# Four short unread products behind each row of 1/rms, the first products by halves of K, and a last scaling that reads its row from the bank

## The chip, the cores and the metric

The kernel runs on one core of one Trainium2 chip. The metric is the device time of one execution in microseconds, from the first to the last instruction with the little that lies around them. Times of single instructions come from one profiled execution, in microseconds from the start of its span.

## The reference, cut to what matters

The input is a sequence of 256 tokens of width 1024. It passes through two layers of a first block and one layer of a second block. Each layer has a mixer between two feed-forward stages or ahead of one. All of them open with the same thing, a root-mean-square norm followed by a matrix product:

```python
def rmsnorm(x, w):
    y = xf * lax.rsqrt(jnp.mean(xf * xf, axis=-1, keepdims=True) + EPS) * w

def swiglu(h, w_gu, w_down):
    gate, up = jnp.split(h @ w_gu, 2, axis=-1)
    return (jax.nn.silu(gate) * up) @ w_down

for layer in range(DEPTH):                      # first block, DEPTH = 2
    x = x + 0.5 * swiglu(rmsnorm(x, ...), ...)
    x = x + mixer(rmsnorm(x, ...))              # gated delta rule, then windowed attention
    x = x + 0.5 * swiglu(rmsnorm(x, ...), ...)
x = rmsnorm(x, final_norm)
# second block: retention and latent attention, merged by two sigmoid gates, then a feed-forward stage
h = h + _mixer(_rmsnorm(h, ...)); h = h + _swiglu(_rmsnorm(h, ...)); return _rmsnorm(h, norm_final_w)
```

There are five feed-forward stages, all with 2,816 inner columns: 22 + 22 blocks of 128 gate and up columns, then 8 blocks of the down matrix over 22 blocks of K (the weight arrays `gu10`, `gu20`, `gu11`, `gu21`, `gu30`).

## The kernel before, in words

The activations lie transposed: 8 tiles `X[0..7]` of 128 features by 256 tokens. Every big product is computed in three parts, for precision: weights and activations are each split into a high part, cast to a narrower format, and a low part, the remainder, and `lin` (lines 373 to 375) issues high by high, low weight by high, high weight by low, for each of the 8 blocks of K. One "column" below is such a set of 24 products (8 x 3), each with 128 x 128 weights loaded and 256 token columns streamed. A feed-forward stage has 44 columns of gate and up and 8 x 66 products of the down matrix, some 1,580 products in all.

A `Stream` brings the weights: `load` starts one transfer of up to 2,048 elements a partition (1 MB, two columns) on SP's queue into one of three buffers, `piece` splits 512 elements of it (half a column) into `whi` on ScalarE (line 355) and `wlo` on VectorE (line 356), with eight buffers of each. `Norm.add` does the same for the activations: `xh` on ScalarE (line 394), `xl` on VectorE (line 395); `accum` squares a tile on ScalarE (403, 406) and adds it up on GpSimd (407).

The norm's factor 1/rms is the same for all features, so it is applied behind the products. `rnorm_nat` sums the squares over the partitions with products that have one column (line 413), VectorE scales them (426), GpSimd takes the power -0.5 (383). `row_bcast` spreads the result over 128 partitions with a product with an identity (435), and VectorE copies it to the tile `r` (437). The next readers are the two multiplications that take a gate and an up column out of their banks (lines 478 and 480).

`opening` orders this for one stage: most of columns a and b, the sums of squares, the rest of a and b, the first block of column c, `row_bcast`, the rest of column c. Seven stages open like this, the first feed-forward stage with other cut points. The banks: pool `ps` has three, pool `pm` five; a feed-forward column takes one of `ps` and gives it back when line 478 or 480 has read it.

The first stage loads the activations in pairs of tiles and its first column in two pieces of half a column. The squares are taken in `squares` after all of the eight `add`. At the end, `row_bcast` gives `r` and three multiplications (line 1534) scale the output tiles, each followed by its transfer.

## Time and profile before

| | |
|---|---|
| median of 3 runs | 1466.39 us (1466.23 to 1467.72) |
| the profiled execution's own time | 1458.11 us |
| its span | 1456.3 us |
| TensorE busy | 1426.7 us, 98% |
| VectorE, ScalarE, GpSimd busy | 1106.2, 858.5, 116.3 us |
| mean granted TensorE clock | 0.995 of full speed |

The busy time counts each product from its start to its modelled end, and products overlap. So the pace of the products is read from the number that start in a stretch, not from the busy share. The profiled execution lies 8.3 us below the median of the runs.

### The profile page before, as it was taken

Reading aid. Unit: us, or ns where it says so; the run is one execution under the profiler, and the core shown is the slowest. Engines: PE = TensorE matmul, PEld = TensorE weight load, DVE = VectorE, ACT = ScalarE, POOL = GpSimd, SP = SyncE. Lnnn points to the kernel's source line nnn. Section 1 sums busy time; section 2 is a strip of 40 time slices with the busy share of each in tenths; the row PEclk is TensorE's granted clock in tenths of the full one; section 3 lists DMA queues with packets and bytes.
Section 4 is the critical chain, followed back from the end, with each engine's and each line's share of the span. In section 5 each row is a group of like instructions: output and inputs, shape, how many; then the busy total and the mean of one; then the engine's idle time right before and its main releaser. Section 6 shows DMA issues by size and latency. Waiting matters only on the chain.

```text
span 1456.3 us, 31032 instructions
## 1 busy us (share of the span) xinstructions
PE 1426.7 (98%) x12318; PEld 1396.2 (96%) x12318; DVE 1106.2 (76%) x2340; ACT 858.5 (59%) x1767; POOL 116.3 (8%) x136
## 2 busy tenths in 40 slices
PE   8999999998999999999999999999999999999997
PEld 8999999998999999999998899999999899999997
DVE  6877667896877766777668877788887868777764
ACT  6555558555655555555556665566545766665552
POOL 2000131011200001000010100013001000100000
PEclk9999999999999999999999999999999999999999
DMA  7655443541456555555552455555333425555551
GB/s 253 227 200 197 159 169 116 169 155 44 156 192 203 186 194 199 184 194 203 188 189 88 145 200 182 198 197 180 123 139 109 145 98 200 197 202 192 189 198 59
DMA packets 46369, 248.35 MB, mean 171 GB/s; under 512 B 11408, under 2 KB 16272, under 8 KB 17168
## 3 DMA queue, kind: packets, MB, share of 16 engines
q1 hardware_dynamic: 45680, 245.87, 49.5%
q8 instruction: 97, 1.59, 0.4%
q10 hardware_dynamic: 544, 0.50, 0.1%
q14 instruction: 48, 0.39, 0.1%
HBM read 243.99 MB, written 2.36 MB: 169 GB/s over the span
## 4 chain that ended last, share of the span: by engine, by line
PE 87%; DVE 7%; ACT 3%; DMA 1%; issue 1%; POOL 1%; SPq 0%; DVEq 0%; POOLq 0%; ACTq 0%
PE bank L373 26%; PE bank L375 26%; PE bank L374 26%; DVE wlo L356 2%; ACT whi L355 1%; DVE cv L652 1%; PE bank L979 1%; PE bank L830 1%; PE bank L1331 1%; PE bank L1136 0%; PE bank L1361 0%; DVE xl L395 0%; PE bank L969 0%; POOL rr L383 0%; DMA xt<-xt 0%
## 5 line engine op out<-in xcount | busy, mean ns | idle before, releaser
L356 DVE TENSOR_TENSOR wlo<-raw,whi 128x512 fp32r<-128x512 f32 x922 | 641.6, 700 | 254.2 <-ACT whi L355 252.7
L355 ACT CAST whi<-raw 128x512 fp32r<-128x512 f32 x922 | 565.5, 619 | 430.4 <-PE bank L375 406.1
L373 PE MATMUL bank<-xh,whi 128*128 128x256 f32 (+1 forms) x2488 | 695.1, 279 | 1.7 <-ACT whi L355 1.0
L374 PE MATMUL bank<-xh,wlo 128*128 128x256 f32 (+1 forms) x2488 | 690.8, 278 | 2.0 <-DVE wlo L356 2.0
L375 PE MATMUL bank<-xl,whi 128*128 128x256 f32 (+1 forms) x2488 | 690.4, 278 | 1.0 <-DVE xl L395 0.9
L373 PEld LDWEIGHTS bank<-xh,whi 128*128 128x128 f32 x2488 | 466.8, 188 | 4.0 <-issue 1.8
L374 PEld LDWEIGHTS bank<-xh,wlo 128*128 128x128 f32 x2488 | 467.0, 188 | 3.2 <-DVE wlo L356 2.8
L375 PEld LDWEIGHTS bank<-xl,whi 128*128 128x128 f32 x2488 | 466.6, 188 | 2.1 <-DVE xl L395 1.6
L375 PE MATMUL bank<-al,whi 128*128 128x256 f32 x880 | 242.9, 276 | 0.0
L373 PE MATMUL bank<-ah,whi 128*128 128x256 f32 x880 | 242.9, 276 | 0.0
L374 PE MATMUL bank<-ah,wlo 128*128 128x256 f32 x880 | 242.9, 276 | 0.0
L373 PEld LDWEIGHTS bank<-ah,whi 128*128 128x128 f32 x880 | 165.2, 188 | 0.0
L374 PEld LDWEIGHTS bank<-ah,wlo 128*128 128x128 f32 x880 | 165.2, 188 | 0.0
L375 PEld LDWEIGHTS bank<-al,whi 128*128 128x128 f32 x880 | 165.2, 188 | 0.0
L407 POOL TENSOR_TENSOR ssq<-sq,ssq 128x256 f32<-128x256 f32 (+1 forms) x72 | 62.9, 874 | 1066.3 <-ACT sq L406 1056.7
L378 ACT CAST ah<-ffu 128x256 fp32r<-128x256 f32 x110 | 44.8, 407 | 26.4 <-DVE ffu L482 26.3
L482 DVE TENSOR_TENSOR ffu<-ffg,ffu 128x256 f32<-128x256 f32 x110 | 46.7, 425 | 4.7 <-ACT ffg L481 1.2
L481 ACT ACTIVATE ffg<-ffg 128x256 f32<-128x256 f32 x110 | 45.4, 414 | 4.0 <-DVE ffg L478 3.7
L478 DVE TENSOR_TENSOR ffg<-bank,r 128x256 f32<-128x256 f32 x110 | 46.6, 424 | 0.9 <-PE bank L375 0.8
L480 DVE TENSOR_TENSOR ffu<-bank,r 128x256 f32<-128x256 f32 x110 | 46.6, 424 | 0.1
L379 DVE TENSOR_TENSOR al<-ffu,ah 128x256 fp32r<-128x256 f32 x110 | 46.0, 418 | 0.6 <-ACT ah L378 0.5
L373 PE MATMUL bank<-dec,whi 128*128 128x256 f32 x128 | 36.8, 287 | 0.0
(368 smaller groups left out, 1429.8 us busy)
## 6 DMA issues: line engine op xcount, KB each, us to landing
raw<-gu SPq DMA_DIRECT2D x109, 1024.0 KB, 4.8
raw<-dn SPq DMA_DIRECT2D x55, 1024.0 KB, 4.8
raw<-wret SPq DMA_DIRECT2D x12, 1024.0 KB, 4.8
raw<-aqk SPq DMA_DIRECT2D x8, 1024.0 KB, 4.7
raw<-wga SPq DMA_DIRECT2D x8, 1024.0 KB, 4.8
raw<-bin SPq DMA_DIRECT2D x6, 1024.0 KB, 4.9
raw<-az SPq DMA_DIRECT2D x4, 1024.0 KB, 4.9
raw<-av SPq DMA_DIRECT2D x4, 1024.0 KB, 5.0
```

Source lines behind the costliest of these rows:

```text
L355: A.copy(hi[:, :n], raw[:, o : o + n])
L356: V.tensor_tensor(lo[:, :n], raw[:, o : o + n], f32(hi[:, :n]), op=ALU.subtract)
L373: mm(o, wh, xh[:, :n], start=k == 0, stop=False)
L374: mm(o, wl, xh[:, :n], start=False, stop=False)
L375: mm(o, wh, xl[:, :n], start=False, stop=k == last)
L378: A.copy(hi, src)
L379: V.tensor_tensor(lo, src, f32(hi), op=ALU.subtract)
L407: G.tensor_tensor(acc[:, :n], q[:, :n], acc[:, :n], op=ALU.add)
L478: V.tensor_tensor(g, pg, r[:, :S], op=ALU.mult)
L480: V.tensor_tensor(u, pu, r[:, :S], op=ALU.mult)
L481: A.activation(g, g, AF.Silu)
L482: V.tensor_tensor(u, g, u, op=ALU.mult)
```

## The change

There are three edits.

First, `settle`: four products with the first 16 of the 128 weight columns of a piece that is split already, and the first activation tile, into a bank that nothing reads. They stand directly behind `row_bcast` in each `opening`, and once more ahead of the gate columns of the second block's mixer, at eight places in all. The first feed-forward stage doesn't use `opening` any more and has none.

Second, the first stage. Its weight chunks are whole (2,048 elements), but the first two are brought in parts, in the order in which they are used. The first three columns are computed by halves of K: the first four blocks of K for the columns 0, 1 and 2, then the last four blocks for each. Then come columns 3, 4 and 5 in banks of `pm`; the squares are spread behind them by one-column copies (`behind`), which only make a square wait for a weight piece. The sums of squares stand in the middle of column 5, and `row_bcast` behind it.

Third, the end. The two halves of the row have a bank each, so that the products of the squares that are there early are all issued ahead of those of the last tile; and the last scaling reads the row from its bank, without the copy to `r`. One small multiplication of constants moves from VectorE to GpSimd.

```diff
+    def settle(st, off, xs):
+        b = bank(pm, [P, 512])
+        wh, _ = st.at(off, P)
+        for i in range(4):
+            mm(b[:16, :S], wh[:, :16], xs[0][0][:, :S], start=True, stop=True)
...
         r = row_bcast(rn, n)
+        settle(*jobs[2][0][1:4])
         c(range(at[1], KD))
...
             if first:
-                first()
-            r = opening(norm, [(pre[i], {}) for i in range(3)], at=(KD - 1, 3) if first else (5, 1))
+                pre = {i: (bank(ps if i < 3 else pm, [P, S]), gu, i * D, norm.xs) for i in range(6)}
+                r = first(lambda i, ks: lin(*pre[i], ks=ks))
...
                 st, stm = Stream("wga"), Stream("wmo")
+                settle(st, 0, xs)
...
+    def first(part):
+        half = range(KD // 2), range(KD // 2, KD)
+        for h in range(2):
+            for i in range(3):
+                for d in half[h]:
+                    if i == 0:
+                        n.add(d, X[d], col("ffn1_norm0", d), square=False)
+                    if d in (0, KD // 2):
+                        gu.piece(2 * i + h)
+        for h in range(2):
+            for i in range(3):
+                part(i, half[h])
+        for h in range(2):
+            part(3 + h, range(KD))
+            for d in half[h]:
+                n.ssq = n.accum(n.ssq, X[d], S, f32(gu.piece((1, 1, 3, 5, 6, 7, 8, 9)[d])[0]))
...
+        part(5, half[0])
+        rn = rnorm_nat(n.ssq, D)
+        part(5, half[1])
+        return row_bcast(rn)
...
-    b = bank(pm, [P, 512])
+    bs = [bank(pm, [P, 512]) for c in range(2)]
+    for i, t in enumerate((fin.ssq, last[0])):
+        for c in range(2):
+            mm(bs[c][:, 0:1], t[:, c * P : c * P + P], ones[:, 0:1], start=i == 0, stop=i == 1)
...
-    r = row_bcast(v)
+    r = bank(pm, [P, 512])
+    for c in range(2):
+        mm(r[:, c * P : c * P + P], v[:, c : c + 1].to_broadcast([P, P]), ident, start=True, stop=True)
```

TensorE at the opening of the second feed-forward stage, before. Names are output<-inputs; `rn` is 1/rms, `bank_5318` the third column:

```order
L375 MATMUL bank_5318<-xl_991_5142,whi_5393 128x256
L435 MATMUL bank_5400<-tabs_81,rn_5376 128x128 x2
L373 MATMUL bank_5318<-xh_993_5148,whi_5393 128x256
L374 MATMUL bank_5318<-xh_993_5148,wlo_5394 128x256
L375 MATMUL bank_5318<-xl_994_5149,whi_5393 128x256
```

The same place in the change, where the third column is `bank_5333`:

```order
L382 MATMUL bank_5333<-xl_990_5157,whi_5408 128x256
L453 MATMUL bank_5415<-tabs_81,rn_5391 128x128 x2
L389 MATMUL bank_5420<-xh_989_5156,whi_5408 16x256 x4
L380 MATMUL bank_5333<-xh_992_5163,whi_5408 128x256
L381 MATMUL bank_5333<-xh_992_5163,wlo_5409 128x256
```

Nothing moved but the four short products, which now stand between the spread of the row and the rest of the column.

VectorE in the first stage around the copy of `r`, before; `bank_162` and `bank_163` are columns 0 and 1:

```order
L426 TENSOR_SCALAR rn_253<-bank_250 128x2
L356 TENSOR_TENSOR wlo_259<-raw_256,whi_258 128x512
L356 TENSOR_TENSOR wlo_280<-raw_256,whi_279 128x512
L437 COPY r_274<-bank_271 128x256
L356 TENSOR_TENSOR wlo_307<-raw_256,whi_306 128x512
L478 TENSOR_TENSOR ffg_295<-bank_162,r_274 128x256
L480 TENSOR_TENSOR ffu_297<-bank_163,r_274 128x256
```

And in the change, where columns 0 and 1 are `bank_126` and `bank_127`:

```order
L444 TENSOR_SCALAR rn_382<-bank_379 128x2
L363 TENSOR_TENSOR wlo_518<-raw_515,whi_517 128x512
L455 COPY r_404<-bank_401 128x256
L363 TENSOR_TENSOR wlo_534<-raw_515,whi_533 128x512
L499 TENSOR_TENSOR ffg_406<-bank_126,r_404 128x256
L501 TENSOR_TENSOR ffu_408<-bank_127,r_404 128x256
```

VectorE's order is the same, one split of weights between the copy and the first reader of a bank. What moved is TensorE's place: before, 21 products of column 2 stand behind the spread of the row; in the change column 6 does, as the next rows show (`bank_131` is column 5, `bank_436` column 6, which takes the bank that column 0 had):

```order
L382 MATMUL bank_131<-xl_41_177,whi_385 128x256
L453 MATMUL bank_401<-tabs_81,rn_382 128x128 x2
L380 MATMUL bank_436<-xh_18_132,whi_439 128x256
L381 MATMUL bank_436<-xh_18_132,wlo_440 128x256
L382 MATMUL bank_436<-xl_19_133,whi_439 128x256
```

## Rows read from the trace of the kernel before

**Rows 1.** The page: the chain that ended last, share of the span by engine.

```profile
PE 87%; DVE 7%; ACT 3%; DMA 1%; issue 1%; POOL 1%; SPq 0%; DVEq 0%; POOLq 0%; ACTq 0%
```

**Rows 2.** Windows, TensorE alone: stretch, its length, busy (products), clock, DMA, GB/s.

```profile
1300.00:1400.00 100.00, 100.00 (x885) 1.00 0.57 192
40.00:48.00 8.00, 8.00 (x73) 1.00 0.88 306
22.40:30.40 8.00, 8.00 (x70) 1.00 0.99 391
```

**Rows 3.** Timeline, TensorE, second feed-forward stage: start, length, engine, line, operation.

```profile
571.23 0.61 PE L435 MATMUL bank<-tabs,rn 128*128 128x128 f32 x4
...
571.59 0.37 PE L373 MATMUL bank<-xh,whi 128*128 128x256 f32 x1
571.79 0.29 PE L374 MATMUL bank<-xh,wlo 128*128 128x256 f32 x1
571.92 0.28 PE L375 MATMUL bank<-xl,whi 128*128 128x256 f32 x1
```

**Rows 4.** Timeline, TensorE, opening of the first mixer, whose column a has 16 columns.

```profile
200.12 0.28 PE L373 MATMUL bank<-xh,whi 128*16 128x256 f32 x1
200.23 0.28 PE L374 MATMUL bank<-xh,wlo 128*16 128x256 f32 x1
200.35 0.28 PE L375 MATMUL bank<-xl,whi 128*16 128x256 f32 x1
200.46 0.28 PE L373 MATMUL bank<-xh,whi 128*128 128x256 f32 x1
```

**Rows 5.** Timeline, TensorE, the first stage.

```profile
7.05 0.45 PE L373 MATMUL bank<-xh,whi 128*128 128x256 f32 x1
...
17.02 0.61 PE L413 MATMUL bank<-ones,ssq 128*128 128x1 f32 x4
...
19.06 0.71 PE L435 MATMUL bank<-tabs,rn 128*128 128x128 f32 x4 [1.21 <-POOL rn L383]
19.53 0.36 PE L374 MATMUL bank<-xh,wlo 128*128 128x256 f32 x1
...
34.40 0.28 PE L373 MATMUL bank<-xh,whi 128*128 128x256 f32 x1
```

**Rows 6.** Groups of instructions from 7 to 34.4 us: the first of lin's three lines.

```profile
L373 PE MATMUL bank<-xh,whi 128*128 128x256 f32 x56 | 16.3, 292 | 1.0 <-ACT whi L355 1.0
```

**Rows 7.** Timeline, ScalarE, the last activation tiles; then groups of the first 22.3 us.

```profile
9.89 0.89 ACT L394 ACTIVATE xh<-xt,colv 128x256 fp32r<-128x256 f32 x2
...
L355 ACT CAST whi<-raw 128x512 fp32r<-128x512 f32 x11 | 6.3, 609 | 0.2 <-DMA raw<-gu 0.2
L356 DVE TENSOR_TENSOR wlo<-raw,whi 128x512 fp32r<-128x512 f32 x8 | 6.0, 766 | 1.9 <-ACT whi L355 1.9
```

**Rows 8.** Windows, all engines: PE, PEld, DVE, ACT, POOL, clock, DMA share, GB/s.

```profile
10.00:12.00 2.00, 1.66 (x13) 1.47 (x12) 1.67 (x4) 1.94 (x5) 1.68 (x2) 1.00 1.02 377
```

**Rows 9.** Timeline, VectorE, behind the spread of the row in the first stage.

```profile
19.81 0.42 DVE L437 COPY r<-bank 128x256 f32<-128x256 f32 x1 [0.77 <-PE bank L435]
...
20.15 0.68 DVE L356 TENSOR_TENSOR wlo<-raw,whi 128x512 fp32r<-128x512 f32 x1
...
20.75 0.42 DVE L478 TENSOR_TENSOR ffg<-bank,r 128x256 f32<-128x256 f32 x1
```

**Rows 10.** Timeline, the end.

```profile
1446.79 0.83 PE L1527 MATMUL bank<-ones,ssq 128*128 128x1 f32 x6 [0.85 <-ACT ssq L403]
...
1449.40 0.42 DVE L437 COPY r<-bank 128x256 f32<-128x256 f32 x1 [1.59 <-PE bank L435]
1449.86 2.43 DVE L1534 TENSOR_TENSOR xt<-xt,r 128x768 f32<-128x768 f32 x3
```

**Rows 11.** The page's costliest groups: one operation from a bank, one not.

```profile
L482 DVE TENSOR_TENSOR ffu<-ffg,ffu 128x256 f32<-128x256 f32 x110 | 46.7, 425 | 4.7 <-ACT ffg L481 1.2
L478 DVE TENSOR_TENSOR ffg<-bank,r 128x256 f32<-128x256 f32 x110 | 46.6, 424 | 0.9 <-PE bank L375 0.8
```

More of the change, by code (lines that the diff above doesn't have):

```diff
@@ L346, in load, with load_part @@
             return self.raw[c]
+        def load_part(self, c, lo, hi):
+            if c not in self.raw:
+                self.raw[c] = sb(wp, [P, CHUNK], "raw")
+            o = self.loads[c][0]
+            nc.sync.dma_start(self.raw[c][:, lo:hi], self.ap[:, o + lo : o + hi])
         def piece(self, j):
@@ L398, in add, with accum @@
                 self.ssq = self.accum(self.ssq, src, n)
-        def accum(self, acc, src, n):
+        def accum(self, acc, src, n, behind=None):
             if acc is None:
                 acc = sb(sp, [P, ST], "ssq")
+                if behind is not None:
+                    V.tensor_copy(acc[:, 0:1], behind[:, 0:1])
                 A.activation(acc[:, :n], src[:, :n], AF.Square)
@@ L405, in accum @@
             q = sb(sp, [P, ST], "sq")
+            if behind is not None:
+                V.tensor_copy(q[:, 0:1], behind[:, 0:1])
             A.activation(q[:, :n], src[:, :n], AF.Square)
@@ L465, in proj @@
                 return bank(ps, [P, S]), gu, i * D, norm.xs
-            pre = {i: proj(i) for i in range(3)}
             if first:
-                first()
-            r = opening(norm, [(pre[i], {}) for i in range(3)], at=(KD - 1, 3) if first else (5, 1))
+                pre = {i: (bank(ps if i < 3 else pm, [P, S]), gu, i * D, norm.xs) for i in range(6)}
+                r = first(lambda i, ks: lin(*pre[i], ks=ks))
+            else:
+                pre = {i: proj(i) for i in range(3)}
+                r = opening(norm, [(pre[i], {}) for i in range(3)])
             for m in range(KF):
@@ L1411, in feed @@
         return after
-    gu = Stream("gu10", sizes=(512, 512, 1024))
-    load_x(nc.sync, 0, 2)
-    A.dma_start(colv, dram["colv"])
-    gu.load(0)
+    gu = Stream("gu10")
+    nc.sync.dma_start(colv[:, :8], dram["colv"][:, :8])
+    load_x(nc.sync, 0, 1)
+    gu.load_part(0, 0, 512)
     A.activation(junk, mhalf, AF.Silu)
@@ L1421 @@
         mm(b[:, :P], ones, ones, start=True, stop=True)
-    load_x(nc.sync, 2, 2)
+    load_x(nc.sync, 1, 3)
+    gu.load_part(0, 1024, 1536)
+    gu.load_part(1, 0, 512)
     load_x(nc.sync, 4, 2)
-    gu.load(1)
     load_x(nc.sync, 6, 2)
-    gu.load(2)
+    gu.load_part(0, 512, 1024)
+    gu.load_part(0, 1536, 2048)
+    gu.load_part(1, 512, 1024)
+    gu.load_part(1, 1024, 2048)
     nc.sync.dma_start(tabs[:, :P], dram["tabs"][:, :P])
+    nc.sync.dma_start(colv[:, 8:], dram["colv"][:, 8:])
     n = cur[0]
-    for d in range(KD):
-        n.add(d, X[d], col("ffn1_norm0", d), square=False)
-        if d in (0, 3):
-            gu.piece(d // 3)
-    def squares():
-        for d in range(KD):
-            n.ssq = n.accum(n.ssq, X[d], S)
+    def first(part):
[14 more added lines that the diff above has]
+                n.ssq = n.accum(n.ssq, X[d], S, f32(gu.piece((1, 1, 3, 5, 6, 7, 8, 9)[d])[0]))
         V.tensor_copy(tabs[:, P : P + 1], n.ssq[:, 0:1])
@@ L1441, in squares @@
         load_rest()
-    ffn("10", n, feed("mix_norm0"), 0.5, None, gu, squares)
+        part(5, half[0])
+        rn = rnorm_nat(n.ssq, D)
+        part(5, half[1])
+        return row_bcast(rn)
+    ffn("10", n, feed("mix_norm0"), 0.5, None, gu, first)
     if dump:
@@ L1460 @@
     wfm = sb(cp, [P, KD], "wfm")
-    V.tensor_tensor(wfm, cols("final_norm"), cols("norm_mix_2"), op=ALU.mult)
+    G.tensor_tensor(wfm, cols("final_norm"), cols("norm_mix_2"), op=ALU.mult)
     mixn = Norm()
@@ L1523 @@
     ffn("30", n, after_fin, 1.0)
-    b = bank(pm, [P, 512])
+    bs = [bank(pm, [P, 512]) for c in range(2)]
+    for i, t in enumerate((fin.ssq, last[0])):
+        for c in range(2):
+            mm(bs[c][:, 0:1], t[:, c * P : c * P + P], ones[:, 0:1], start=i == 0, stop=i == 1)
+    v = sb(sp, [P, 4], "rn", bufs=4)
     for c in range(2):
-        for i, t in enumerate((fin.ssq, last[0])):
-            mm(b[:, c : c + 1], t[:, c * P : c * P + P], ones[:, 0:1], start=i == 0, stop=i == 1)
-    v = sb(sp, [P, 4], "rn", bufs=4)
-    V.tensor_scalar(v[:, :2], b[:, :2], 1.0 / D, EPS, op0=ALU.mult, op1=ALU.add)
+        V.tensor_scalar(v[:, c : c + 1], bs[c][:, 0:1], 1.0 / D, EPS, op0=ALU.mult, op1=ALU.add)
     rsq(v[:, :2], 2)
-    r = row_bcast(v)
+    r = bank(pm, [P, 512])
+    for c in range(2):
+        mm(r[:, c * P : c * P + P], v[:, c : c + 1].to_broadcast([P, P]), ident, start=True, stop=True)
     od = out.rearrange("(k p) t -> p k t", p=P)
```

## The prediction

> **What bounds the kernel now.** I read the chain that ended last first: 87% of it is TensorE, and nearly all of that the three lines of `lin` [rows 1]. So the end moves with the number of products, with their pace, and with the places where TensorE stands. What is worth reading next is the pace, from windows that count the products that begin. A 100 us window deep in the last feed-forward stage holds 885; some 2.5 of these only reach in over an edge, so one begins every 0.1133 us [rows 2]. Most of the kernel looks like this, but not all: 8 us of the first stage hold 73 products at 40 us and 70 at 22.4 us, at the same full clock and with no wait between them [rows 2]. With the same 2.5 taken off that is 0.1135 and 0.1185. There are two paces, 4 to 5 ns apart; I use 4.5. A stretch keeps its pace until something interrupts it. A feed-forward stretch of some 1,560 products costs 1,560 x 0.0045 = 7.0 us more at the slow pace.
>
> The profiled execution took 1458.11 us, the runs 1466.39 in the median. The gap of 8.28 us is large beside the spread of the three runs (1.5 us). The profiled execution has its long stretches at the fast pace (the spread of the row in the second stage is followed by steps of 0.20, 0.13 and then the fast pace [rows 3]; the window of the last stage is fast [rows 2]). One long stretch at the slow pace in the timed runs would make 7.0 of the 8.28 us. No trace here shows a timed run, so this stays an inference; it decides the forecast.
>
> Last I read the first stage by its timeline. Its first product begins at 7.05 us, the first of the eighth column at 34.40 [rows 5]. Between them lie 7 x 24 = 168 products (56 on each line [rows 6]), worth 19.0 us at 0.1133. So 8.3 us are lost there: waits for weights and activations, 2.04 us from the sums of squares to the spread of the row with little to do between [rows 5], the slow pace, and a stall at the seventh column.
>
> **The short products.** There are eight places of four products, 32 in all. They stream 256 columns each. A product with 16 weight columns began 0.11 or 0.12 us after the one ahead of it, as a full one does [rows 4]. At 0.1133 that is 32 x 0.1133 = 3.6 us, on the engine that bounds. The least: the first product behind the spread of the row is followed only after 0.20 us [rows 3]; if shorter weight loads there save 0.09 each time, 2.9 us remain. The mixers' openings and the gates hide a little where TensorE then waits anyway. I take +3.3 us, between 2.9 and 3.6.
>
> What they may give back is the pace behind them. Rows speak on both sides. In the first mixer's opening three such products stood in a slow stretch; the steps were 0.11, 0.12 and 0.11, a little shorter than around them, but the full products behind them went on slowly [rows 4]. In the second stage, one step of 0.13 behind the spread of the row was followed by the fast pace [rows 3]. Four products with light loads are a longer interruption than that one step. I take it that a long stretch then begins at the fast pace where it would have begun at the slow one: 0 in the profiled execution, where these stretches are fast already, and -7.0 us in the timed runs. Bounds: 0 and -8.3.
>
> The Trainium skill bears against this. "TensorE: Matmul & The Clock Gate", section "Back-to-back issue gap", gives one gap for a full clock, N / 2.4 GHz + 2.5 ns, which makes 109 ns for 256 columns, and no second pace. By it nothing could be settled, and the eight places would cost 32 x 0.109 = 3.5 us for nothing. The windows differ from it: 113.3 and some 118 ns at the full clock [rows 2].
>
> **The first stage.** In the change the first half-column and one activation tile are loaded first, so the first product is again ready by the end of the 14 warming products, at about 7.05 us [rows 5]. The first halves of columns 0 to 2 need four activation tiles and three half-columns; the next limit is the second half. Before, the last two tiles were converted from 9.89 to 10.78 us [rows 7], behind 1.68 MB of transfers. Now 1.84 MB lie ahead of them and 0.26 MB more until the first half-column of the second half: at 377 GB/s [rows 8] tiles are 0.4 us later and that piece is there some 0.7 us behind them. ScalarE splits it by about 11.5 (0.61 us), VectorE by 12.2 (0.7 us) [rows 7]. From there TensorE should have no wait: 35 + 72 products at 0.116, between the paces, are 12.4 us; the sums of squares add 0.5. That is 25.1, and a wait of up to 0.2 us for 1/rms follows, since the way from the sums to the spread takes 2.04 us [rows 5] and 12 products with the sums 1.9. The spread of the row begins at 25.3.
>
> Here is the price of the new order. Column 6 needs the bank of column 0, which is free when VectorE has multiplied it by `r`. In the old order 21 products of column 2 covered that; now nothing does. Before, the spread began at 19.06, the copy at 19.81, the split of weights that stands between at 20.15, and the multiplication ran from 20.75 to 21.17 [rows 5, 9]. So TensorE stands from 0.47 us (19.06 to 19.53) to about 2.16 us behind the start of the spread: 1.7 us of stall, in the same VectorE order as before. Column 6 begins at 27.5, and with 24 products and a start like others behind a wait (0.2 us) the eighth column begins at 30.4. Against 34.40 that is **-4.0 us**; -5 if the transfers come 1 us earlier, -3 if they come later. The squares are done by about 21.4 by my sum, so they don't bound. What comes behind in the order (the three waiting pairs of evacuations on VectorE, 4 us) has 2 x 2.7 us of columns to hide in; each column's bank is read in time.
>
> **The end.** The chain there is 6 passes of sums of squares behind the last square, 0.83 us [rows 10]; now 4 passes, -0.22. The copy to `r` goes: 1449.40 to 1449.86, -0.46 [rows 10]. A second small VectorE instruction adds up to 0.1. The scaling now reads a bank: operations of one shape take 424 ns from a bank and 425 without [rows 11], so 0, or at most 0.1 for each of three. Sum -0.6, between -0.3 and -0.7. The skill's "VectorE: DVE Perf Modes", section "Rules for kernel authors", says to copy to SBUF first if there are many operations on a product's output; here are three, and by that advice the 0.46 would not be gained. The multiplication of constants on GpSimd waits for a late transfer, behind squares that are early; nothing hangs on it.
>
> **The sum.** +3.3 - 4.0 - 0.6 = -1.3 us with all paces as profiled: 1456.8 of the profiled execution's own time, 1465.1 of the median. With one stretch of a stage brought from the slow pace to the fast one, -8.3: **1458.1 us**. A measurement of this kernel tells 0.2%, 2.9 us, from no change.
>
> **The rivals.** *No pace changes* (1465.1): the gap of 8.28 us has another cause, or the short products leave the paces alone, as three did [rows 4]. For it: the profiled stretches are fast already. Against: something must make the 8.28 us. Its chance, 0.22, includes that the skill's single gap holds.
>
> *The first stage stays slow* (1458.1 + 6.3 = 1464.4): it has no short products, and 1,416 products follow its new stall, 6.3 us at 4.5 ns. Before, the one spread that had waited for GpSimd [rows 5] was followed by the slow pace [rows 2], until a stall ended it. For it: the wait of up to 0.2 us is there again. Against: now a stall of 1.7 us follows at once, and the pace is set anew. 0.14.
>
> *The other side: the short products leave long stretches at the slow pace.* If the pace behind them is the slow one, where it was fast, each stage adds 7.0: one makes 1472.1, four some 1493. It decides from one stage on, since 1465.1 + 7.0 is 0.4% over the median. For it: the full products behind three short ones were slow [rows 4]. Against: they were slow ahead of them too. 0.14.
>
> *The start gains nothing* (about 1462 with one stretch made fast, 1469 without): the second half's pieces come 2 us later than I sum, with a stall longer than 1.7. 0.06.
>
> **How the numbers follow.** The forecast has 0.44, and its own range is 1455.5 to 1460.5 (start -5 to -3, short products 2.9 to 3.6, up to 8.3 of the gap). The range that holds 8 in 10 runs from 1455.5 to 1470.5: it takes in the first two rivals and most of the last, and leaves out most of the other side. Faster by over 0.2% means below 1463.5: 0.44, a third of the second rival, a part of the first and last, 0.54. Slower means above 1469.3: 0.14 with what the last and the first stage add where no stretch is made fast, 0.19. Between: 0.27.
>
> **What would show it.** In the changed profile: four products of 16 columns behind each spread, about 0.11 us apart, and 885 products in 100 us in every feed-forward stage; a first stage whose eighth column begins near 30.4 and whose TensorE waits some 1.7 us for VectorE ahead of column 6; an end 0.6 us shorter from the last square. The median should then lie within 3 us of the profiled execution. The forecast is wrong if the gap between profile and median stays 8 us, or if a stage shows 850 products in 100 us.

## The result, and the profile after

The changed kernel takes **1481.09 us** in the median (1480.33 to 1487.69), the kernel before 1466.36: a ratio of **1.0119, 95% interval 1.0083 to 1.0154**. It is slower by 14.7 us where 8.3 less were forecast. Its profiled execution took 1487.69 us with a span of 1484.6, 28.3 us more than the span of before. The profiles differ by more than the medians for two reasons: the runs of before lie 8.3 us above its profiled execution, and the profiled execution of the change is its slowest, 6.6 us above its median.

The page of the changed kernel begins like that of before: TensorE is busy for nearly all of the span, with 32 more products, and the chain is TensorE.

```profile
PE 1455.2 (98%) x12350; PEld 1424.1 (96%) x12350; DVE 1110.5 (75%) x2347; ACT 859.0 (58%) x1767; POOL 115.7 (8%) x137
...
PE 89%; DVE 5%; ACT 2%; issue 1%; POOL 1%; DMA 0%; SPq 0%; DVEq 0%; POOLq 0%; ACTq 0%
```

So the pace is read next, in a window deep in each of the four feed-forward stages that open with a spread and short products (stretch, length, busy and products, clock, DMA, GB/s), as in [rows 2]:

```profile
440.00:540.00 100.00, 100.00 (x885) 1.00 0.57 191
640.00:740.00 100.00, 100.00 (x852) 1.00 0.55 188
900.00:1000.00 100.00, 100.00 (x851) 1.00 0.54 183
1340.00:1440.00 100.00, 100.00 (x851) 1.00 0.55 187
```

Three of four stages run at 851 or 852 in 100 us. In the profile of before, such windows show 884 or 885 in all four. The clock is full in each of them, and TensorE never stands. Three stretches of 1,569, 1,533 and 1,533 products at 4.5 ns more are 20.9 us of the 28.3; the short products are some 3.6. Some 4 us more lie in the first mixer (from the spread of the second opening to that of the third it is 193.5 us, in before 189.6), where the granted clock was at half for 17.1 us in three stretches, against 6.8 us in two in before; the rows stand below with the first stage.

The place where the pace is set, ahead of the third feed-forward stage (TensorE's timeline: start, length, line; a row with x4 is four products):

```profile
575.85 0.28 PE L382 MATMUL bank<-xl,whi 128*128 128x256 f32 x1
575.97 0.61 PE L453 MATMUL bank<-tabs,rn 128*128 128x128 f32 x4
576.33 0.71 PE L389 MATMUL bank<-xh,whi 128*16 128x256 f32 x4
576.88 0.28 PE L380 MATMUL bank<-xh,whi 128*128 128x256 f32 x1
576.99 0.28 PE L381 MATMUL bank<-xh,wlo 128*128 128x256 f32 x1
577.11 0.28 PE L382 MATMUL bank<-xl,whi 128*128 128x256 f32 x1
577.23 0.28 PE L380 MATMUL bank<-xh,whi 128*128 128x256 f32 x1
```

The four short products take 0.55 us up to the next full one, and the full ones go on at 0.118 for the 1,569 that follow. In before the same place went over to 0.113 (the rows headed second feed-forward stage, [rows 3], stand by their time, 571.23 us, at this third one).

The first stage of the changed kernel, TensorE at four places:

```profile
25.06 0.28 PE L382 MATMUL bank<-xl,whi 128*128 128x256 f32 x1
27.02 0.71 PE L453 MATMUL bank<-tabs,rn 128*128 128x128 f32 x4 [1.69 <-POOL rn L397]
29.28 0.55 PE L380 MATMUL bank<-xh,whi 128*128 128x256 f32 x1 [1.54 <-DVE ffg L499]
...
34.53 0.41 PE L380 MATMUL bank<-xh,whi 128*128 128x256 f32 x1
```

The last product of columns 0 to 5 begins at 25.06, then TensorE stands for 4.2 us but for the spread itself; the seventh column begins at 29.28 and the eighth at 34.53, where before had 34.40 [rows 5]. In the thirteen kernels that keep the first stage of before the eighth column begins between 32.86 and 35.53, so a difference of a microsecond between two profiles says little here. VectorE in that time:

```profile
23.05 0.15 DVE L1476 COPY tabs<-ssq 128x1 f32<-128x1 f32 x1 [1.46 <-POOL ssq L425]
...
23.24 2.49 DVE L363 TENSOR_TENSOR wlo<-raw,whi 128x512 fp32r<-128x512 f32 x4
25.65 0.15 DVE L444 TENSOR_SCALAR rn<-bank 128x2 f32<-128x2 f32 x1
...
27.77 0.42 DVE L455 COPY r<-bank 128x256 f32<-128x256 f32 x1 [1.37 <-PE bank L453]
28.11 0.68 DVE L363 TENSOR_TENSOR wlo<-raw,whi 128x512 fp32r<-128x512 f32 x1
28.71 0.42 DVE L499 TENSOR_TENSOR ffg<-bank,r 128x256 f32<-128x256 f32 x1
```

The small copies that release the late transfers hold VectorE until the sums are there, four splits follow that could have been done in that time, and only then comes 1/rms. Windows of the seventh column and of three stretches in the first mixer (TensorE alone) show the clock:

```profile
29.30:34.50 5.20, 5.20 (x24) 0.50 0.87 353
212.50:215.80 3.30, 3.30 (x17) 0.50 0.34 144
273.90:280.70 6.80, 6.58 (x28) 0.50 0.46 154
311.40:318.20 6.80, 6.80 (x64) 0.50 0.36 114
```

After the stand of 4.2 us the granted clock was 0.50, the level of 1.2 GHz, and the 24 products of the seventh column took 5.25 us instead of 2.7 to 2.8. In the first mixer of before it was at half in two stretches:

```profile
212.00:215.40 3.40, 3.40 (x18) 0.50 0.39 164
334.90:338.30 3.40, 3.40 (x19) 0.50 0.00 0
```

Over the 20 profiles of this case the first mixer takes between 185.5 us (e13, never at half) and 195.1 us (e11, 20.5 us at half), and its length goes with the time at half (correlation 0.88, 0.42 us more for each microsecond at half). So, beside the pace, the clock goes with differences of several microseconds between executions; which of the two, a longer mixer or a longer time at half, brings the other is not shown.

The end, timeline rows of ScalarE and VectorE from the last square on:

```profile
1475.23 0.42 ACT L419 ACTIVATE ssq<-xt 128x256 f32<-128x256 f32 x1 [7.29 <-DVE xt L514]
...
1478.08 2.42 DVE L1579 TENSOR_TENSOR xt<-xt,bank 128x768 f32<-128x768 f32 x3 [1.59 <-PE bank L1576]
```

From the last square to the end of the span it is 1484.6 - 1475.23 = 9.4 us. In the trace of before the last square begins at 1446.32, and the span ends 10.0 us later. Over all profiles it is 9.3 to 9.4 us in seven of the nine kernels with the new end and 9.9 in two, and 10.0 to 10.1 in eight of the eleven with the old one and 10.5 to 10.9 in three. The scaling takes 2.42 from the bank and took 2.43 from SBUF [rows 10].

### The profile page after: what moved, and what is told of

Read it like the earlier page. It is cut to its first block, busy times and chain, and to the rows that moved or that the text cites. A ratio compares the mean times of both kernels' runs of the same rounds, so it can differ in the third digit from the quotient of the medians.

```text
span 1484.6 us, 31111 instructions
## 1 busy us (share of the span) xinstructions
PE 1455.2 (98%) x12350; PEld 1424.1 (96%) x12350; DVE 1110.5 (75%) x2347; ACT 859.0 (58%) x1767; POOL 115.7 (8%) x137
## 4 chain that ended last, share of the span: by engine, by line
PE 89%; DVE 5%; ACT 2%; issue 1%; POOL 1%; DMA 0%; SPq 0%; DVEq 0%; POOLq 0%; ACTq 0%
PE bank L380 27%; PE bank L382 27%; PE bank L381 27%; DVE wlo L363 2%; ACT whi L362 1%; PE bank L1000 1%; PE bank L1352 0%; PE bank L851 0%; PE bank L1157 0%; PE bank L1382 0%; PE bank L728 0%; DVE xl L409 0%; PE bank L990 0%; PE bank L701 0%; PE bank L1370 0%
## 5 line engine op out<-in xcount | busy, mean ns | idle before, releaser
L382 PE MATMUL bank<-xl,whi 128*128 128x256 f32 (+1 forms) x2488 | 698.5, 281 | 1.1 <-DVE xl L409 1.0
L381 PE MATMUL bank<-xh,wlo 128*128 128x256 f32 (+1 forms) x2488 | 698.7, 281 | 0.2 <-DVE wlo L363 0.2
L382 PEld LDWEIGHTS bank<-xl,whi 128*128 128x128 f32 x2488 | 474.3, 191 | 2.4 <-DVE xl L409 1.9
```

Of the source, the lines that this page charges most:

```text
L381: mm(o, wl, xh[:, :n], start=False, stop=False)
L382: mm(o, wh, xl[:, :n], start=False, stop=k == last)
```

## The experiments

"Stages" are the products in 100 us of the windows above, from the one profiled execution of each kernel; 884 and 885 are the fast pace, 851 and 852 the slow one. The first feed-forward stage, which has no short products in any kernel but e8, is not among them; it ran at the slow pace in the profiles of e13 and e24 alone. Medians of before belong to the runs beside which a kernel was timed: they were taken on other chips and differ by up to 7 us.

| kernel | short products | stages | median, before's | ratio (95%) |
|---|---|---|---|---|
| the change | 4 of 16 | 885 852 851 851 | 1481.09, 1466.36 | 1.0119 (1.0083 to 1.0154) |
| e1 change without them | none | 885 885 851 885 | 1463.80, 1465.34 | 0.9975 (0.9943 to 1.0007) |
| e2 before with them | 4 of 16 | 852 885 851 851 | 1480.35, 1465.34 | 1.0105 (1.0067 to 1.0143) |
| e3 | 4 of 128 | 885 885 884 885 | 1464.25, 1465.34 | 1.0000 (0.9963 to 1.0036) |
| e4 new end alone | none | 851 885 885 885 | 1462.08, 1465.34 | 0.9972 (0.9940 to 1.0004) |
| e5 ahead of the spread | 4 of 16 | 852 851 851 852 | 1491.30, 1469.36 | 1.0140 (1.0080 to 1.0201) |
| e6 | 1 of 16 | 851 885 885 885 | 1465.89, 1469.36 | 0.9959 (0.9926 to 0.9992) |
| e8 midway | 4 of 16 | 851 885 852 885 | 1467.97, 1469.36 | 1.0011 (0.9971 to 1.0051) |
| e9 change, copies late | none | 852 885 884 885 | 1463.12, 1469.36 | 0.9986 (0.9950 to 1.0021) |
| e7 | 8 of 16 | 885 885 885 885 | 1465.32, 1472.34 | 0.9956 (0.9934 to 0.9978) |
| e10 | 4 of 64 | 884 884 885 884 | 1470.88, 1472.34 | 0.9973 (0.9944 to 1.0002) |
| e13 six products on | 4 of 16 | 852 885 885 885 | 1469.34, 1472.34 | 0.9962 (0.9928 to 0.9996) |
| e11 e9 with full ones | 4 of 128 | 851 885 852 884 | 1472.09, 1472.34 | 1.0006 (0.9972 to 1.0039) |
| e14 the change | 8 of 16 | 885 885 885 885 | 1468.74, 1468.01 | 1.0020 (0.9990 to 1.0049) |
| e15 e9 with eight | 8 of 16 | 884 884 885 884 | 1465.72, 1468.01 | 0.9998 (0.9976 to 1.0019) |
| e16 | 6 of 16 | 885 885 884 885 | 1462.89, 1468.01 | 0.9968 (0.9937 to 1.0000) |
| e18 | 2 of 16 | 884 884 885 885 | 1457.82, 1468.01 | 0.9948 (0.9921 to 0.9974) |
| e21 e18, new end | 2 of 16 | 885 885 885 885 | 1457.06, 1469.73 | 0.9917 (0.9885 to 0.9950) |
| e24 e21, new start | 2 of 16 | 885 885 885 885 | 1457.79, 1469.73 | 0.9910 (0.9877 to 0.9942) |

**Which part loses.** Two theories: the short products leave stretches at the slow pace, or the loss lies in the first stage. e1 takes the products out of the change:

```diff
         r = row_bcast(rn, n)
-        settle(*jobs[2][0][1:4])
...
-                settle(st, 0, xs)
```

> The kernel after without its eight places of four unread products; the new first stage and the new end are kept. Theory A (the short products leave long stretches at the slow pace): the stretches behind the spreads of the row are back at 885 products in 100 us, the span falls by 3.5 us for the products and about 7 us for each of the three feed-forward stages that were slow, and the time is that of before within 3 us, 1463.5 to 1469.5. Rival B (the loss lies in the first stage, with its 4.2 us stall and the half clock behind it): the time stays within 4 us of the change's, 1477 to 1482. Under A the eighth column still begins near 34.5 us, as the start gained nothing.

e2 puts them alone into the kernel before, with the same two lines added (the first stage left out).

> The kernel before with nothing but the eight places of four unread products of 16 weight columns. Theory A: 3.5 us for the products and some 7 us for each long stretch that they leave at the slow pace, two to four of them, so 1477 to 1495; the profile shows about 850 products in 100 us in at least two feed-forward stages. Rival B (the loss lies in the first stage): 1470, only the products' own 3.5 us, and 885 in 100 us in every feed-forward stage behind them.

e1 came back to before, e2 went to the change's time: 15.0 us over before, and three stages at 851 or 852 in its profile. The first theory holds and the second falls. One stage of e1 was slow without any short product. Its opening on TensorE:

```profile
833.80 0.28 PE L380 MATMUL bank<-xh,whi 128*128 128x256 f32 x1
...
834.71 0.28 PE L382 MATMUL bank<-xl,whi 128*128 128x256 f32 x1
834.83 0.60 PE L453 MATMUL bank<-tabs,rn 128*128 128x128 f32 x4
835.19 0.36 PE L380 MATMUL bank<-xh,whi 128*128 128x256 f32 x1
...
835.51 0.28 PE L382 MATMUL bank<-xl,whi 128*128 128x256 f32 x1
...
836.45 0.28 PE L381 MATMUL bank<-xh,wlo 128*128 128x256 f32 x1
```

Ahead of the spread eight steps take 0.91 us, 0.114 each; behind it eight take 0.94, 0.1175. The spread of the row exchanged the two paces. Worked out in the same way for the five kernels that have no short products at a spread (before, e1, e4, e8, e9), over the six places where full products stand on both sides: 25 spreads had the slow pace ahead and the fast one behind, 5 the fast one ahead and the slow one behind, none kept its pace. Two places in other kernels did keep the slow one, one each in e11 and e13 below (in e13 up to its short products).

A closer mark stands inside the spread. Of the steps between its four products the second is 110 ns at all nine places that went on slowly in the eight kernels without narrow products next to the spread (before, e1, e3, e4, e8, e9, e11, e13), those two among them, and 111 or 112 at all 39 that went on fast. So the pace behind shows itself before the spread is over, and the pace ahead tells it only in most places.

**Which property of the products.** e3 has all 128 columns, e10 has 64:

```diff
-            mm(b[:16, :S], wh[:, :16], xs[0][0][:, :S], start=True, stop=True)
+            mm(b[:, :S], wh, xs[0][0][:, :S], start=True, stop=True)
```

> The kernel before with the same eight places of four unread products, but with all 128 weight columns instead of 16. If the light load of 16 columns sets the slow pace (A1), full-width products cost their 3.6 us alone: 1470, and every feed-forward stage runs at 885 products in 100 us as before. If any four products of another kind between the spread and the stretch shift it (A2), some stretches run slow as in the kernel after: 1477 to 1495. Under rival B (the first stage) 1470 again, but then the run with 16 columns stands there too.

> The kernel before with four unread products of 64 weight columns in each of the eight places, between the 16 that made stages slow and the 128 that did not. If the pace hangs on the load being shorter than a full one, some stages are slow, 1474 to 1482; if only very short loads do it, 1466 to 1469 and 885 in 100 us in every feed-forward stage.

In e3 no stage is slow, so full products did no harm there (A1). All its openings were at the slow pace ahead of the spread, so the exchange alone explains it. But e11, below, has the same full products and two slow stages, one behind an opening at the fast pace and one not: full products neither harm nor help. With 64 columns no stage is slow; the median, 1.5 us under before's, lies a little above the 1469 expected for that. A load shorter than a full one is not enough to make a stage slow.

**Which place.** The four ahead of the gates stay as in e2 in e5 and e13; e8 has none there. e5 puts the four ahead of the spread:

```diff
         c(range(at[1]))
+        settle(*jobs[2][0][1:4])
         r = row_bcast(rn, n)
```

e8 has them in the middle of a stage, behind the tenth column, and nowhere else:

```diff
                         lin(*pre[i])
+                        if i == 9:
+                            settle(*pre[i][1:4])
```

e13 has them six full products behind the spread:

```diff
-        c(range(at[1], KD))
+        c(range(at[1], KD - 5))
+        settle(*jobs[2][0][1:4])
+        c(range(KD - 5, KD))
```

In e13 the retention mixer's opening, which has other cut points, adds two blocks of K of its third column twice (six products more, and another result); all other stages compute what they did in before.

> The kernel before with the four unread products of 16 columns ahead of each spread of the row instead of behind it (and ahead of the gates as before). Theory P (the spread's own products set the fast pace, and narrow products right behind them undo it): here nothing narrow stands between the spread and the stretch, so the stretches stay fast, 885 products in 100 us, and only the products' own 3.5 us are paid, 1469. Rival Q (narrow products disturb the pace wherever they stand): two or more slow feed-forward stages, 1477 or more.

> The kernel before with four unread products of 16 columns in the middle of a running stretch, behind the tenth column of each of the five feed-forward stages, and none behind a spread. Theory P (only what follows the spread's fp32 products sets the pace): the pace is the same on both sides of them, and 20 products cost 2.3 us: 1468. Rival Q (narrow products disturb the pace wherever they stand): in some stages the fast pace ends there, each some 1,320 products by 4.5 ns, 6 us: 1474 or more.

> The kernel before with the four products of 16 columns six full products behind each spread (two activation tiles) instead of directly behind it. Theory R (only next to the spread's fp32 products does a narrow load set the pace): the pace is chosen before they come and they leave it, as midway in a stretch; 885 in 100 us in the stages whose opening was slow ahead of the spread, and 1469 with the products' own 3.5 us. Rival (narrow products anywhere in an opening do it): 1477 or more.

Theory P fell: ahead of the spread the four are worse than behind it, with all four stages slow. Its rival Q fell too. Two stages of e8, windows ahead of and behind the short products:

```profile
395.00:415.00 20.00, 20.00 (x172) 1.00 0.53 183
418.00:518.00 100.00, 100.00 (x851) 1.00 0.52 187
584.00:602.00 18.00, 18.00 (x161) 1.00 0.57 199
606.00:706.00 100.00, 100.00 (x885) 1.00 0.55 195
```

With 2.5 taken off, 169.5 in 20 us are 0.118 and 158.5 in 18 us 0.1136: the slow stage was slow and the fast one fast before the four came, and in all five stages they changed nothing. So the place counts: beside the spread's products. In e13 five of six such openings kept the pace that they had ahead of the four; in one it went from slow to fast at them, so six products are not always far enough.

**How many.** e6 has one, e18 two, e16 six, e7 eight, with `range(4)` in `settle` changed to that number.

> The kernel before with one unread product of 16 columns behind each spread instead of four. If the narrow load next to the spread is what does it, one is enough: stretches at 850 products in 100 us and 1474 to 1490. If four are needed (the alignment drifts over several short loads), the stretches stay fast and the time is 1466, since eight products cost 0.9 us.

> The kernel before with eight unread products of 16 columns in each of the eight places instead of four. Theory R (the pace is set where TensorE comes back from the fp32 products of the spread, and a narrow load next to that place shifts it): as with four, at least two long stretches run at 850 products in 100 us; with 7.3 us for 64 products that is 1483 or more. Rival (four is an unlucky count, since one left most stretches fast): with eight the stretches are fast and only the products' 7 us are paid, 1473.

> The kernel before with six products of 16 columns in each place instead of four. Theory S: with eight the steps behind the spread were 200, 116, 113, 119, 117, 113 and then even, so six end just where the fast pace begins: at most one slow feed-forward stage, 1465 to 1471 with 5.4 us for the products. Rival (even counts below eight are bad): two or more slow stages, 1477 or more.

> The kernel before with two products of 16 columns in each place. Theory S: the full loads come in at the third step, inside the change-over, so the pace can fall either way; 1466 to 1480, and at least one slow feed-forward stage that one product would not have made. Rival (four alone is bad): no slow stage behind a spread that follows a slow stretch, 1467.

One left one stage slow, behind a spread with the 110 ns step, where stages without short products went slowly too; two, six and eight none. The theory R (a narrow load beside the spread makes the slow pace) expected 1483 or more from eight and got 1465.3: it falls, and the count decides. The theory S (four end in the middle of the change-over) was right on six and eight and wrong on two, for which it expected a slow stage. The third feed-forward stage with two, and with eight:

```profile
569.67 0.48 PE L382 MATMUL bank<-xh,whi 128*16 128x256 f32 x2
569.99 0.28 PE L373 MATMUL bank<-xh,whi 128*128 128x256 f32 x1
570.11 0.28 PE L374 MATMUL bank<-xh,wlo 128*128 128x256 f32 x1
570.23 0.28 PE L375 MATMUL bank<-xl,whi 128*128 128x256 f32 x1
570.35 0.28 PE L373 MATMUL bank<-xh,whi 128*128 128x256 f32 x1
570.46 0.28 PE L374 MATMUL bank<-xh,wlo 128*128 128x256 f32 x1
```

```profile
576.31 1.17 PE L382 MATMUL bank<-xh,whi 128*16 128x256 f32 x8
577.32 0.28 PE L373 MATMUL bank<-xh,whi 128*128 128x256 f32 x1
577.43 0.28 PE L374 MATMUL bank<-xh,wlo 128*128 128x256 f32 x1
```

With two, three full steps of 0.12 follow and then 0.11; with eight the full products begin at 0.11 at once. With four, in the rows of the change above, they go on at 0.11 and 0.12 and stay at 0.118. Over the kernels with two, six or eight (e7, e14, e15, e16, e18, e21, e24) all 28 stages were fast. In 25 of them the slow pace stood ahead of the spread, where the exchange alone mostly leads to the fast one; in three the fast one stood there, which without short products was followed by the slow one each time. By the closer mark seven of the 28 (two in e7, two in e18, one each in e14, e15 and e24) had the step of 109 or 110 ns behind which the kernels without narrow products there went on slowly, and all seven went on fast; so did two in e10. With four of 16 columns it is the other way round: of the six stages of the change and e2 with 111 or 112 ns there, five went on slowly. These are counts from one profile of each kernel. They fit what two are worth: 16 products cost 16 x 0.1133 = 1.8 us, and the stage that otherwise falls to the slow pace, 5 of 20 in the five kernels without short products at a spread and so about one to a run, does so no more. 7.0 - 1.8 = 5.2 is that estimate; e18 is 7.6 us under before (0.52%). The times by themselves don't single out two. One product (e6) is 0.41% under before, with an interval that overlaps that of e18. Eight cost 7.3 us, which would use up the 7.0, and e7 is 6.5 us under before all the same, while e14, with the same count and the same stages, is level with it; their intervals don't overlap. What separates those two, the start and the end or the chips, is not shown, so differences of some tenths of a per cent between rows of the table from different chips are not to be read as effects of the count.

**The count in the changed kernel.** e14 is the change with eight, e11 the change with full products and with the late copies behind the row.

> The kernel after with eight products of 16 columns in each of its eight places instead of four, all else as in the change. Theory S (four end in the middle of the change-over, eight behind it): 885 products in 100 us in every feed-forward stage, and in spite of 3.6 us more for products a time of 1461 to 1469, 12 to 20 us below the change. Rival (the change's surroundings, its new start among them, make the slow stages): 1477 or more.

> The kernel after with two edits: the eight places of four products with all 128 columns instead of 16, and the late copies behind the row. Theory R: the slow stages of the change vanish with the narrow loads alone, 885 in 100 us in every feed-forward stage; with 2 to 4 us less at the start and at the end and up to 3.6 us more for the products the time is that of before within 5 us, 1461 to 1469, and some 15 us below the change. Rival (in the changed kernel the slow stages have another cause, its new start among them): 1475 or more.

e14 has no slow stage and stands at before, 12.3 us below the change by its median: four is what the change suffered from. e11 came out at before too (1.0006), but with two slow stages in its profile: the expectation's 885 everywhere is wrong, full products don't decide the pace.

**The end and the start.** e4 has the end alone, e9 the change without short products and with the three copies and the late transfers moved:

```diff
-        V.tensor_copy(tabs[:, P : P + 1], n.ssq[:, 0:1])
...
-        load_rest()
         part(5, half[0])
         rn = rnorm_nat(n.ssq, D)
         part(5, half[1])
-        return row_bcast(rn)
+        r = row_bcast(rn)
+        V.tensor_copy(tabs[:, P : P + 1], r[:, 0:1])
...
+        load_rest()
+        return r
```

> The kernel before with the new end alone (two banks, four passes of sums of squares, the scaling read from its bank). Theory: from the last square to the end 0.6 us less than the 9.98 us of before, time 1465.8, no difference that the runs can tell. Rival: reading the bank costs what the copy had, and the end takes the same 9.98 us.

> The kernel after without short products, and with the three small copies that release the late transfers behind the row instead of ahead of the four splits. Theory: the 4.2 us stall ahead of the seventh column is VectorE's order (the copies wait 1.5 us for the sums, four splits of 2.5 us follow, and only then comes 1/rms); with the copies out of the way the spread of the row begins at 25.2 instead of 27.0, the stall is 2.4 us, the eighth column begins 1.8 us earlier, at 32.7, and the time is 1462, with no difference from before that the runs can tell. Rival: the splits wait for ScalarE, 1/rms comes as late as before, and the eighth column begins at 34.5.

e4's time can't be told from before's, as expected, and its end, 1460.7 - 1451.4 = 9.3 us from the last square, is the one expected. In e9 the spread begins at 26.80 and the eighth column at 32.05; TensorE stands for 3.6 us ahead of the seventh. Of the 1.8 us expected from the copies 0.2 came at the spread and 0.6 at the stand: without them VectorE does six splits in a row from 20.73 to 25.43, and 1/rms stands behind them as before, so the rival was right on the order. In the other kernels with either order the spread came at 27.4 (e1 and e14, as in the change) and at 26.8 and 27.1 (e11 and e15, as in e9), so the copies bring some tenths. What came back at the eighth column, 2.5 us, is mostly the clock: it stayed at 1.00 through the seventh column in this execution. e24 also binds the squares to earlier splits and puts the sums ahead of column 5:

```diff
-                n.ssq = n.accum(n.ssq, X[d], S, f32(gu.piece((1, 1, 3, 5, 6, 7, 8, 9)[d])[0]))
+                n.ssq = n.accum(n.ssq, X[d], S, f32(gu.piece((1, 1, 3, 5, 5, 5, 6, 7)[d])[0]))
...
-        part(5, half[0])
         rn = rnorm_nat(n.ssq, D)
-        part(5, half[1])
+        part(5, range(KD))
```

> The kernel after with eight products of 16 columns in each place, and with the three late copies behind the row. Theory S and the start together: all long stretches at 885 in 100 us, the eighth column 2 to 4 us earlier than in before, the end 0.6 us shorter, 7.3 us paid for 64 products: 1458 to 1464, a few tenths of a per cent below before. Rival (the pace behind the spread falls by chance whatever the count): 1470 or more in the median.

> The kernel before with two products of 16 columns in each place and the new end, its first stage unchanged. If two products hold the fast pace behind each spread, every feed-forward stage shows 885 products in 100 us in the profile and the median is 7 to 9 us under that of before, with 0.6 of them from the end. Rival (the gain with two was luck of those runs): within 3 us of before.

> The kernel after with two products of 16 columns in each place, its squares bound to earlier splits, the sums of squares multiplied ahead of the sixth column, and the three late copies behind the row. Theory: 1/rms no longer stands behind four splits, so the spread of the row follows the sixth column at once and TensorE waits about 1.7 us for the bank of column 0, as the prediction had it, instead of 4.2; 2 to 3 us less up to the eighth column than before and 10 to 12 us less in all. Rival: the wait ahead of the seventh column stays above 3 us, since the row's copy stands behind splits, and the time is that of the kernel with two products and the old start.

```profile
26.68 0.28 PE L382 MATMUL bank<-xl,whi 128*128 128x256 f32 x1
26.80 0.60 PE L453 MATMUL bank<-tabs,rn 128*128 128x128 f32 x4
29.12 0.36 PE L380 MATMUL bank<-xh,whi 128*128 128x256 f32 x1 [1.72 <-DVE ffg L499]
...
32.02 0.28 PE L380 MATMUL bank<-xh,whi 128*128 128x256 f32 x1
```

In e24 TensorE's timeline has no wait ahead of the spread any more, and 2.3 us from it to the seventh column; the eighth begins at 32.02. But the stage behind it ran at the slow pace in this profile (682 products from 100 to 180 us, 708 in the change), 6.3 us longer up to the next spread than in e21, so that the 1.5 us against e21 (33.49) was more than given back there. The two cannot be told apart by their medians. Both lie 0.8 to 0.9% below before, and so below the change. e15 misses its range by 1.7 us: with eight, the start brings it to before and not below.

## Why the prediction was wrong, point by point

*The step that failed is the sentence "I take it that a long stretch then begins at the fast pace where it would have begun at the slow one".* The direction was a guess between rows of both signs, and with four products it was the wrong one: three of four stages ran at the slow pace, and so did three in e2, which has nothing but the short products. The rival of the other side, "the short products leave long stretches at the slow pace", is what happened; it had 0.14, and the prediction had named 850 products in 100 us as its sign. Its price was right: 7.0 us a stage, three stages, and 1.0 in the second mixer, behind the spread at 763.88. The evidence used for and against it was of the wrong kind. [Rows 4] show short products in the middle of a slow opening, and e8 shows that away from the spread they do nothing either way; they could not bear on what four do beside it. [Rows 3] were read as one uneven step that brings the fast pace; what they show, with e1, is that the spread as a rule exchanges the paces.

*The gap of 8.28 us* was read as one stretch at the slow pace in the timed runs. That reading fits in size: in kernels without short products at the spread, 5 of 20 stages were slow in the profile, about one to a run, and two products, with which none was slow in three profiles, brought 7.6 us net (e18). It stays an inference, since the timed runs have no traces, and the clock is a rival that the prediction did not name: in the first mixer alone it goes with differences of up to 9 us. In four of five sets of runs of before the time falls as the mean granted clock of the run rises, with correlations of -0.33 to -0.61 (in the fifth it is 0.24), so the clock carries a part of the spread, and most of it is something else. And the three runs of before that agreed within 1.5 us did not show how it varies; 30 runs of the same kernel beside e1 to e4 lie between 1455.67 and 1476.41.

*The skill's single gap.* The Trainium skill, "TensorE: Matmul & The Clock Gate", section "Back-to-back issue gap", has a formula for the gap of an isolated product at full clock, 109 ns for 256 columns. The prediction took it for the pace of a stream; for that the section says that loads and products set the spacing together, and it gives 81 ns at 128 columns and 131 ns at 512, none at 256, and no second pace. The windows at full clock show 113.3 and 117.8 ns, each for over 1,500 products; the measurement decides. By the formula nothing would have been lost but the products' own time.

*Short products +3.3.* At the third stage four took 0.55 us; without them the first full product would have had the step of 0.20 [rows 3] in place of 0.113, so 0.46 net. For eight such places that is 3.7, an estimate from this one, just above the range of 2.9 to 3.6.

*The first stage, -4.0, came out at +0.1.* The last product of column 5 began at 25.06 (their end was forecast at 25.1), and the stall from the start of the spread to the seventh column was 2.26 us (forecast 2.16). Two terms were missing. The spread came at 27.0 and not at 25.3: the squares were done at 23.0 and not at 21.4, since each waits for a split (bound to earlier splits in e24, they were done at 20.6), and four splits stood ahead of 1/rms on VectorE. And after the 4.2 us stand the clock was at half, so the seventh column took 5.25 us instead of 2.9. 1.7 and 2.4 make the 4.1. The first is the order of the change; the second came in five of the seven kernels with the new start, and neither in e9, which stood for 3.6 us, nor in e24. The rival "the start gains nothing" (0.06) is what happened, by another cause than the transfers that it named.

*The end, -0.6,* was right: 9.4 us against 10.0. The same holds for reading the bank: 2.42 and 2.43. The Trainium skill, "VectorE: DVE Perf Modes", section "Rules for kernel authors", leaves the choice between reading a product at the slower rate and, for many operations, copying it to SBUF first; the prediction took three for many. For these three the trace shows no slower read, and the copy's 0.46 went.

Open is why four products of 16 columns, and not two, six or eight, or four of 64, leave the slow pace behind them, and what keeps one of two paces for 1,500 products. The traces show the order of the steps, not what TensorE's weight loads wait for inside.

## What to carry to other kernels

Where the same products run at two paces, count the products that begin in windows of several stages and of several kernels before a forecast hangs on the pace; one profile and three runs don't show how often each occurs. A few unread products where TensorE comes back from a small fp32 product can hold the better pace, but their number has to be measured: added alone to the kernel before, four cost 1.05%, two came out 0.5% under it, one, six and eight 0.3 to 0.4% under, and eight in the changed kernel level with it. Two kernels timed on different chips are not told apart by some tenths of a per cent. When a stall is removed from the products' side, follow the other engine's row order to the instruction that ends it; here small copies and splits in VectorE's order set the end of the stall, not the products.

## What the runs showed of the hardware

- Two paces at full clock, 113.3 and 117.8 ns for products of 128 x 128 weights by 256 columns, kept without change for 1,569 products and more. The four small fp32 products of the spread exchanged them 30 times out of 30 in the five kernels without short products there; e11 and e13 have one place each that stayed slow. The second step inside the spread, 110 ns or 111 to 112, told the pace behind it in 48 places of 48 with no narrow products next to it.
- A product with 16 weight columns has a load of 92 to 98 ns in the trace of the change, where a full one has 188 in the median, and begins no sooner than a full one; in a running stretch it takes on the stretch's pace, 113 or 118 ns.
- The granted clock went to 0.50 during or behind the stand of 3.5 to 4.2 us in the first stage in five of six kernels that had it (the change, e1, e11, e14, e15; not in e9), for 3.4 or 6.8 us, and not in e24, where the stand was 2.4 us. The long stand is not needed for it: with the first stage of before, where the gap ahead of the spread is 1.6 us in all thirteen kernels, e2, e8, e13 and e16 had it behind that gap, and the other nine had not. What brings it is not shown.
- In the first mixer the granted clock was at 0.50 for 0 to 20.5 us, and the mixer took 185.5 to 195.1 us, 0.42 us more for each microsecond at half.
